# Short matmuls of constants at the head of the feed-forward up tiles of a two-layer hybrid decoder

## The chip, the cores and the metric

The kernel runs on one core of one Trainium2 chip. The metric is the device time in microseconds of one execution. Names of engines in the profile: PE is the matmul unit TensorE, PEld its weight loads, DVE is VectorE, ACT is ScalarE, POOL is GpSimd, and SP is SyncE, whose queue issues the DMAs.

## What is computed

256 tokens of width 1024 pass two layers. A layer is a half-step SwiGLU feed-forward, a mixer (stick-breaking attention in layer 0, an RG-LRU recurrent block in layer 1), and a second half-step feed-forward. Each of the six sub-layers normalises its input and modulates it by vectors made from a conditioning vector:

```python
def sublayer_input(x, g, mod_j):
    shift, scale, gate = mod_j[:, 0], mod_j[:, 1], mod_j[:, 2]
    h = rmsnorm(x, g) * (1 + scale[:, None, :]) + shift[:, None, :]
    return h, (1 + gate)[:, None, :]

def swiglu(h, w_gu, w_down):
    g, u = jnp.split(h @ w_gu, 2, axis=-1)
    return (jax.nn.silu(g) * u) @ w_down
...
        x = x + MACARON_W * g * swiglu(h, ffn_w_gu[layer, 0], ffn_w_down[layer, 0])
```

The hidden width of a feed-forward is 2816, 22 tiles of 128. Everything is float32.

## The kernel before

Activations stand with features on the 128 partitions and the 256 tokens in the columns. A product of float32 accuracy is made from three float32r matmuls: weights are split into a high part `wh` (ScalarE, L497) and a rest `wl` (VectorE, L500), activations likewise, and `group` (matmul at L526) adds wh·xh, wh·xl and wl·xh into one bank. A few products use TensorE's own float32 passes instead (`group32`, L543, and the norm's sum over partitions at L608).

A feed-forward has up tiles and a down projection. An up tile (`up`) makes one of the 22 hidden tiles: gate half and linear half side by side in one PSUM bank, eight pieces of the input each, three matmuls a piece, 2 x 8 x 3 = 48 matmuls of 256 columns, each with its own load of 128 x 128 weights. The first eight tiles of the first layer are run together, piece by piece, while their weights arrive; in the three other feed-forwards the first two tiles go through `up_first`, which starts before the norm is known, with 258 columns. That leaves 14 + 20 + 20 + 20 = 74 up tiles made by the loop in `ffn`. `swiglu_tile` then empties the bank, and `down` (also L526) sums all hidden tiles into x.

In the attention, L836 makes values, L902 scores on 64 rows of the array, L905 adds a mask by a bf16 matmul with the identity (256 columns), L929 and L931 sum over keys with constant triangles (384 and 128 columns), and L951 applies the weights. The constants that the change uses are there already: `ident` and `mask` in bf16, `ones` in float32, `ntri` and `none_` in float32r.

The order on each engine is made by a list scheduler in the kernel. Every operation is entered with an engine, a cost in ns, what it reads and what it writes; TensorE's operations get due times in program order (`nominal`, the running sum of their costs), and the others are sorted by when TensorE needs what they make. Weights arrive by DMA (L472) into 3 raw buffers; there are 7 buffers each for `wh` and `wl` of 1024 columns, and 8 banks.

Of the kernel before, what the change touches and what calls it, by code (L numbers as in the profile page):

```python
# [12 lines left out]
PSUM = bass.MemoryType.PSUM  # L13

P = 128
T = 256
TX = T + 2
D = 1024
KD = D // P
# [5 lines left out]
S = 384  # L25
# [19 lines left out]
NPAR = OFF_LAM + NR  # L45
NP0 = OFF_MB + 3 * KD  # what the first sub-layer needs

# [12 lines left out]

# [1 line left out]
class Space:  # L62
    """Memory that buffers take turns in, in program order: equal slots or an arena of cells."""

# [41 lines left out]
class Program:  # L106
# [58 lines left out]
    def schedule(self):  # L165
        ops = self.ops
        for o in ops:
            for d, data in o.deps.items():
                d.succ.append((o, data))
        # a buffer's users hold up whoever needs its place next  # L170
        spaces = {b.space for o in ops for b in o.bufs if b.space is not None}
# [33 lines left out]
        busy, gap, loads = 0.0, None, self.loads  # L205
        late = 0.0  # how far TensorE is behind its own time
        queue = {e: sorted((o for o in ops if o.eng == e), key=lambda o: (o.prio, o.seq)) for e in ("ACT", "DVE")}
# [4 lines left out]
        def guess(o, depth):  # L212
            """when an operation might start, from its inputs alone"""
            t = 0.0
            for d, data in o.deps.items():
                if d.start is not None:
                    t = max(t, d.end + self.lag(d, o, data))
                elif depth == 0:
                    return None
                else:  # L220
                    g = guess(d, depth - 1)
                    if g is None:
                        return None
                    t = max(t, max(g, free[d.eng]) + d.cost + self.lag(d, o, data))
            return t

        def wait_for(e, t, o):
            """an urgent operation, soon ready, that a start of o at t would hold up"""
            q = queue[e]
            while head[e] < len(q) and q[head[e]].start is not None:  # L230
                head[e] += 1
            n, i = 0, head[e]
            slack = o.prio + late - t
            while n < LOOK and i < len(q):
                u = q[i]
                i += 1
                if u.start is not None:
                    continue
                n += 1
                if u is o or u.prio >= o.prio:  # L240
                    break
                g = guess(u, 3)
                if g is None or g >= t + o.cost or g <= t:
                    continue
                if u.prio + late - g < o.cost and u.prio + late - g < slack - MARGIN:
                    return g
            return None
# [17 lines left out]
        while len(order) < len(ops):  # L265
# [60 lines left out]
            for b in o.bufs:  # L326
                b.uses -= 1
                if b.uses == 0 and b.space is not None:
                    sp = b.space
                    sp.live -= 1  # L330
                    # in-order engines: earlier readers on other engines have ended by their own time
                    t = o.end + 120.0 if b.hist else o.end
                    b.rel = max(getattr(b, "rel", 0.0), t)
                    for i in range(b.at, b.at + b.n):
                        sp.free[i] = b.rel
                    sp.last = max(sp.last, b.rel)
                else:
                    b.rel = max(getattr(b, "rel", 0.0), o.end + 120.0)
# [26 lines left out]
def trunk(ctx, tc, xT, cb, par, modw, gu0, gu, wdn, qk, wv, wo, win, wri, wout, out):  # L365
# [10 lines left out]

# [1 line left out]
    def ring(name, n, cols, dt=F32, pl=const):  # L378
# [52 lines left out]

# [1 line left out]
    def fixed(name, cols, dt=F32):  # L433
# [35 lines left out]

# [1 line left out]
    def dma(dst, src, n, w, after=(), lat=None):  # L471
# [10 lines left out]
    def load(src, n, name, chain=None, size=HALF):  # L482
        """n columns of weights: returns pieces of size columns, each (hi, lo)."""
        raw = Buf(rawr, name=f"raw_{name}")
# [22 lines left out]
    class Acc:  # L507
        """regions of one PSUM bank, with one start flag for the bank"""

# [4 lines left out]
        def group(self, part, o, w, wc, xs, xc, stop, parts=(None,), passes=(0, 1, 2)):  # L514
            """o += w[:, wc].T @ xs[:, xc] in three exact products"""
            b = self.b
# [21 lines left out]
    def group32(acc, part, o, w, wc, x32, xc, n, stop):  # L538
        """the same product, by TensorE's own float32 passes"""
        b = acc.b  # L540
# [8 lines left out]

# [1 line left out]
    mraw, mfin = {}, {}  # L551

    def mod_tile(l, s, w, t, after=(), lat=None):
        """row tile t of mod_w[l] for sub-layer s, part w (0 shift, 1 scale, 2 gate)."""
        key = (l, s, w)
# [12 lines left out]
    def mod_final(l, s, w, t0=0, n=KD):  # L568
# [4 lines left out]
        pp = [(pars, 0)] if l == s == 0 else [pars]  # L573
        mi = lambda: m()[:, t0 : t0 + n]  # noqa: E731
        fo = lambda: f()[:, t0 : t0 + n]  # noqa: E731
        if w == 0:
# [9 lines left out]

# [1 line left out]
    ssq, hcur, gcur = {}, {}, {}  # L588
# [27 lines left out]
    def scaled(gen, d):  # L616
        """x * scale and, in two more columns, the shift: what the first tile works on before the norm is known"""
        gs, sh = mfin[gen + (1,)], mfin[gen + (0,)]
        hi, lo = Buf(hxr), Buf(hxr)
        gcur.setdefault(gen, []).append((hi, lo))  # L620
        c = slice(d, d + 1)
        shc = lambda: sh()[:, c].to_broadcast([P, 2])  # noqa: E731
        A(lambda: hi()[:, T:], shc, AF.Copy, 2, [(sh, d)], [(hi, 1)])
# [19 lines left out]
    def down(l, s, nxt, srcs, ys, nlast, hook=None, post=None, n32=0):  # L643
        """x += gate * (W.T y) and what the next norm needs; srcs: chunks of two k tiles [P, 2, D];
        ys(k): (hi, lo), or one float32 tile for the first n32 chunks, and its columns."""
        accs = [Acc(f"acc_{l}_{s}_{i}") for i in range(5)]
# [5 lines left out]
        def step(d, k):  # L652
            acc, j = place[d]
            y, yc = ys(k)
            o = lambda b: b[:, j * T : (j + 1) * T]  # noqa: E731
            if k < 2 * n32:
# [33 lines left out]
        for ds in ((0, 1), (2, 3), (4, 5), (6,), (7,)):  # L690
# [3 lines left out]
            for d in ds:  # L694
                residual(d)

    def up(acc, ws, hx_):
        """acc = two regions of T columns: pieces of w [k, 2 P] against h"""
        for k in range(KD):
# [5 lines left out]
    def up_first(gen, ws, scale=(1.0, 1.0)):  # L705
        """the same products for the first tiles, on x * scale and shift: for each tile and region
        (tile, normed), column to add, its dependency"""
        gx = gcur.pop(gen)
# [20 lines left out]

# [1 line left out]
    def swiglu_tile(acc, y):  # L731
# [10 lines left out]
    def ffn(l, s, nxt, hook):  # L742
# [55 lines left out]
        for f in range(f0, NF):  # L798
            hook(f)
            acc = Acc(f"g_{j}_{f}")  # L800
            up(acc, load(gu[j, f], CH, f"gu_{j}_{f}", chained if j == 0 and f == f0 else None), hcur[l, s])
            swiglu_tile(acc, tile_out())
        down(l, s, nxt, [wdn[j, :, 2 * c : 2 * c + 2, :].rearrange("p k d -> p (k d)") for c in range(NF // 2)],
             lambda k: (ys[k], slice(0, T)), 2, lambda c: hook(NF + 2 * c))

# [1 line left out]
    def attention(l, s, nxt, hook):  # L807
        R, F = new_phase(88, 24)
        # softplus(-lambda) for the recurrent block, with the same tables
        A(lam, lambda: col(OFF_LAM, NR), AF.Abs, NR, [pars], [lam], after=[pr.last_pe])  # L810
# [68 lines left out]

        W2 = 2 * S  # for each of two heads: block 0 (t = 0..255), block 1 (t = 128..255)  # L880
        BL = (slice(0, T), slice(T, S))
# [7 lines left out]
        def scores(f):  # L889
            """rows are keys s, columns queries t"""  # L890
            qh, ql = qs.pop(f)
# [49 lines left out]
        def values(f):  # L941
# [13 lines left out]
            for e in range(2):  # L955
                rows = slice(e * 64, (e + 1) * 64)
                bi = lambda e=e, rows=rows: b()[rows, e * T : (e + 1) * T]  # noqa: E731
                A(lambda rows=rows: oh()[rows, :], bi, AF.Copy, T, [b], [(oh, e)], psum=True)
# [29 lines left out]

# [1 line left out]
    def rglru(l, s, nxt):  # L990
        N32 = 1  # chunks of w_out that float32 passes take
        R, F = new_phase(8 * (NB - N32), 86)
# [137 lines left out]

# [1 line left out]
    last = []  # L1132
# [73 lines left out]

# [1 line left out]
    order = pr.schedule()  # L1208
# [58 lines left out]
```

## Time and profile before

| what | value |
|---|---|
| median of the runs | 997.18 us (2 runs, 996.13 and 998.24) |
| span of the profiled execution, first to last instruction | 994.6 us |
| TensorE busy | 980.2 us (99%), 8096 matmul records |
| VectorE busy | 798.5 us (80%) |
| ScalarE busy | 561.8 us (56%) |
| HBM read | 248.92 MB |
| mean granted TensorE clock | 0.998 |

The profile describes one execution, and its page gives the span alone as that execution's time; the median lies 2.6 us above it. Busy shares are the union of overlapping records: a matmul's record is longer than the step to the next one, so the pace is read from starts, not from record lengths. The view of waits gives who waited for whom, the total, the number of times and the longest; the chain that ended last is the path from the last instruction back to the first.

### The profile page before, as it was taken

How to read it: one execution, taken by the hardware profiler on the slowest of the kernel's cores; microseconds unless marked ns; L12 is line 12 of the kernel's file. 1: busy time of each engine (PE TensorE's matmuls, PEld its weight loads, DVE VectorE, ACT ScalarE, POOL GpSimd, SP SyncE). 2: the span in 40 equal slices, each digit the busy share in tenths (PEclk: the TensorE clock that was granted, in tenths of full speed). 3: DMA queues.
4: the chain of work that ended last, by engine and by line, in shares of the span. 5: the costliest groups of instructions: out<-in, count | busy, mean ns of one | idle time of the engine just before them, and what ended most of it. 6: DMA issues, size and time to landing. Idle time of an engine off the chain costs nothing.

```text
span 994.6 us, 19696 instructions
## 1 busy us (share of the span) xinstructions
PE 980.2 (99%) x8096; PEld 969.1 (97%) x8096; DVE 798.5 (80%) x1316; ACT 561.8 (56%) x902; POOL 2.2 (0%) x14
## 2 busy tenths in 40 slices
PE   7999999999999999999999999999999999999997
PEld 5999999999999999999999999999999999999996
DVE  7997887898988999888789989874997996555433
ACT  5475443379776854444366544443779785444333
POOL 0000000000000000000000000000000000000000
PEclk9999999999999999999999999999999999999999
DMA  9988898845666389899866988886334645545421
GB/s 341 358 317 316 326 331 304 338 166 193 241 232 234 143 307 334 328 343 336 313 266 254 333 326 334 335 308 214 107 134 163 254 176 210 205 174 191 165 111 43
DMA packets 48331, 251.24 MB, mean 253 GB/s; under 512 B 5489, under 2 KB 6129, under 8 KB 28530
## 3 DMA queue, kind: packets, MB, share of 16 engines
q1 hardware_dynamic: 48242, 249.99, 68.0%
q8 instruction: 63, 1.03, 0.4%
q14 instruction: 26, 0.21, 0.1%
HBM read 248.92 MB, written 1.05 MB: 251 GB/s over the span
## 4 chain that ended last, share of the span: by engine, by line
PE 98%; DVE 1%; DMA 0%; issue 0%; ACT 0%; SPq 0%; DVEq 0%
PE bank L526 90%; PE bank L836 2%; PE bank L902 1%; PE bank L1025 1%; PE bank L951 1%; PE bank L543 1%; PE bank L929 1%; DMA x<-in_xT 0%; PE bank L905 0%; PE bank L608 0%; PE bank L931 0%; DVE x L1124 0%; DVE ssq L1151 0%; DVE rawm L564 0%; DVEq L1262 0%
## 5 line engine op out<-in xcount | busy, mean ns | idle before, releaser
L526 PE MATMUL bank<-hx,wh 128*128 128x256 f32 (+1 forms) x3392 | 606.9, 282 | 2.5 <-ACT hx L476 2.5
L497 ACT ACTIVATE wh<-raw 128x1024 fp32r<-128x1024 f32 (+1 forms) x328 | 337.2, 1046 | 339.2 <-PE bank L526 238.3
L526 PEld LDWEIGHTS bank<-hx,wh 128*128 128x128 f32 x3392 | 520.7, 189 | 4.1 <-ACT hx L476 3.3
L500 DVE TENSOR_TENSOR wl<-raw,wh 128x1024 fp32r<-128x1024 f32 (+1 forms) x328 | 390.1, 1209 | 129.4 <-ACT wh L497 126.0
L526 PE MATMUL bank<-hx,wl 128*128 128x256 f32 (+1 forms) x1696 | 475.3, 280 | 0.0
L526 PEld LDWEIGHTS bank<-hx,wl 128*128 128x128 f32 x1696 | 320.5, 189 | 0.0
L526 PE MATMUL bank<-arenar,wh 128*128 128x256 f32 x1664 | 294.7, 280 | 0.0
L526 PEld LDWEIGHTS bank<-arenar,wh 128*128 128x128 f32 x1664 | 254.1, 188 | 0.1
L526 PE MATMUL bank<-arenar,wl 128*128 128x256 f32 x832 | 232.4, 279 | 0.0
L564 DVE SCALAR_TENSOR_TENSOR rawm<-rawm,cact 128x1024 f32<-128x1024 f32 x144 | 174.8, 1219 | 19.7 <-DMA rawm<-in_modw 19.3
L526 PEld LDWEIGHTS bank<-arenar,wl 128*128 128x128 f32 x832 | 156.1, 188 | 0.0
L476 ACT ACTIVATE arenar<-a 128x256 fp32r<-128x256 f32 x88 | 35.3, 404 | 4.4 <-DVE a L735 4.4
L740 DVE TENSOR_TENSOR arenar<-a,arenar 128x256 fp32r<-128x256 f32 x88 | 36.4, 418 | 0.5 <-ACT arenar L476 0.5
L735 DVE TENSOR_TENSOR a<-bank,sg 128x256 f32<-128x256 f32 x82 | 34.1, 418 | 0.1
L476 ACT ACTIVATE sg<-bank 128x256 f32<-128x256 f32 x82 | 30.2, 368 | 6.4 <-PE bank L526 4.8
L476 ACT ACTIVATE hx<-hpre,mf 128x256 fp32r<-128x256 f32 x48 | 23.3, 501 | 16.5 <-DVE mf L577 11.1
L666 DVE SCALAR_TENSOR_TENSOR x<-bank,mf,x 128x256 f32<-128x256 f32 x48 | 21.7, 478 | 11.2 <-PE bank L526 10.8
L476 ACT ACTIVATE hx<-x,mf 128x256 fp32r<-128x256 f32 x40 | 19.0, 502 | 18.2 <-DVE x L666 18.2
L636 DVE SCALAR_TENSOR_TENSOR hx<-hpre,mf,hx 128x256 fp32r<-128x256 f32 x48 | 22.7, 479 | 2.1 <-ACT hx L476 2.1
L836 PE MATMUL bank<-wh,hx 128*128 128x256 f32 x128 | 23.7, 282 | 0.0
L476 ACT ACTIVATE arenaf<-arenaf 128x768 f32<-128x768 f32 (+1 forms) x31 | 22.0, 737 | 0.5
L634 DVE SCALAR_TENSOR_TENSOR hpre<-x,mf,rst 128x256 f32<-128x256 f32 x48 | 21.6, 479 | 0.6 <-ACT rst L476 0.4
(97 smaller groups left out, 467.7 us busy)
## 6 DMA issues: line engine op xcount, KB each, us to landing
raw<-in_gu SPq DMA_DIRECT2D x79, 1024.0 KB, 5.2
rawm<-in_modw SPq DMA_DIRECT2D x144, 512.0 KB, 6.0
raw<-in_wdn SPq DMA_DIRECT2D x44, 1024.0 KB, 4.8
raw<-in_win SPq DMA_DIRECT2D x10, 1024.0 KB, 4.8
raw<-in_qk SPq DMA_DIRECT2D x8, 1024.0 KB, 5.3
raw<-in_gu SPq DMA_DIRECT2D x14, 512.0 KB, 6.0
raw<-in_wout SPq DMA_DIRECT2D x5, 1024.0 KB, 4.9
raw<-in_wv SPq DMA_DIRECT2D x4, 1024.0 KB, 7.0
```

What stands on the lines that cost most here:

```text
L476: act.activation(o(), i(), f, **{k: (v() if callable(v) else v) for k, v in kw.items()})
L497: act.activation(h()[:, :m], raw()[:, a : a + m], AF.Copy)
L500: dve.tensor_tensor(lo()[:, :m], raw()[:, a : a + m], f32(h()[:, :m]), ALU.subtract)
L526: pe.matmul(o(b()), wc(u()), xc(v()), start=start and n == 0, stop=stop and n == len(passes) - 1, skip_group_check=True)
L543: pr.op("PE", c_mm(n, 4), lambda: pe.matmul(o(b()), wc(w()), xc(x32()), start=start, stop=stop, skip_group_check=True), [w, x32] + ([] if ...
L564: dve.scalar_tensor_tensor(raw(), raw(), 1.0, cact(), ALU.mult, ALU.mult, accum_out=m()[:, t : t + 1])
L634: V(lambda: dve.scalar_tensor_tensor(hp(), x[d](), gs()[:, c], q(), ALU.mult, ALU.mult), T, [x[d], (gs, d), q], [hp], ptr=1)
L636: V(lambda: dve.scalar_tensor_tensor(lo()[:, :T], hp(), sh()[:, c], f32(hi()[:, :T]), ALU.add, ALU.subtract), T, [hp, (sh, d), hi], [lo], ...
L666: dve.scalar_tensor_tensor(x[d](), acc.b()[:, j * T : (j + 1) * T], gate()[:, d : d + 1], x[d](), ALU.mult, ALU.add)
L735: V(lambda: dve.tensor_tensor(a(), b()[:, T:], sg(), ALU.mult), T, [(b, (1, 0)), sg], [a])
L740: V(lambda: dve.tensor_tensor(y[1](), a(), f32(y[0]()), ALU.subtract), n, [a, y[0]], [y[1]])
L836: pe.matmul(o, u()[:, tb * P : (tb + 1) * P], v()[:, c0 : c0 + 256], start=start and n == 0, stop=k == KD - 1 and n == 2, skip_group_check ...
```

## The change

A table `SHORT` has one entry for each of the 88 tiles of the four feed-forwards (22 each). Just ahead of the 48 matmuls of an up tile, the new function `short` enters a TensorE operation that writes one or several small products of constants into the tile's bank; the first of the 48 then starts the bank anew, so the products are thrown away. The kinds: "b" bf16 identity times n columns of the mask; "h" the same on 64 rows; "f" float32 ones; "r" float32r triangles; "m" several bf16 matmuls one after the other. Of the 74 tiles of the loop, 70 get an entry that is not empty: 14 in the first feed-forward, 19, 19 and 18 in the others. The comments of the file are stripped too, which moves line numbers only: L526 of before is L534 of after, for instance.

```diff
+SHORT = [(None, 0)] * 8
+SHORT += [("b", n) for n in range(1, 15)]
+SHORT += [(None, 0)] * 3 + [("b", n) for n in (15, 16, 17, 31, 33, 47, 49, 63, 65, 95, 97, 127, 129, 255)] + [("h", n) for n in (1, 2, 3, 4, 65)]
+SHORT += [(None, 0)] * 3 + [("f", n) for n in range(1, 11)] + [("r", n) for n in (2, 4, 6, 8, 10, 12, 34, 66, 98)]
+SHORT += [(None, 0)] * 3 + [("m", n) for n in ((1, 1), (1, 1, 1), (1, 2), (3, 3, 3), (5, 5, 5, 5), (7,) * 8, (65, 65), (33,) * 3, (129,) * 2,
+                                               (128, 1), (1, 128), (64, 63), (255, 255))] + [("b", 1), ("b", 3), ("f", 1), (None, 0), ("b", 2), ("b", 1)]
...
+    def short(acc, i):
+        kind, n = SHORT[i]
+        if kind is None:
+            return
+        def fn():
+            o = acc.b()
+            if kind == "b":
+                pe.matmul(o[:, :n], ident, mask[:, :n], start=True, stop=True)
+            elif kind == "h":
+                pe.matmul(o[:, :n], ident[:64, :], mask[:64, :n], start=True, stop=True)
+            elif kind == "f":
+                pe.matmul(o[:, :n], ones, ones[:, :n], start=True, stop=True)
+            elif kind == "r":
+                pe.matmul(o[:, :n], ntri, none_[:, :n], start=True, stop=True)
+            else:
+                for m in n:
+                    pe.matmul(o[:, :m], ident, mask[:, :m], start=True, stop=True)
+        pr.op("PE", 120.0, fn, [], [acc.b])
...
         for f in range(f0, NF):
             hook(f)
             acc = Acc(f"g_{j}_{f}")
+            short(acc, j * NF + f)
             up(acc, load(gu[j, f], CH, f"gu_{j}_{f}", chained if j == 0 and f == f0 else None), hcur[l, s])
             swiglu_tile(acc, tile_out())
```

TensorE at the head of the first up tile of the loop in the first feed-forward (tile 8, entry "b" with one column), before:

```order
L526 MATMUL bank_65<-hx_105,wh_82 128x256
L526 MATMUL bank_65<-hx_106,wh_82 128x256
L526 MATMUL bank_65<-hx_105,wl_89 128x256
L526 MATMUL bank_66<-hx_91,wh_83 128x256
L526 MATMUL bank_66<-hx_92,wh_83 128x256
```

And now:

```order
L534 MATMUL bank_65<-hx_105,wh_82 128x256
L534 MATMUL bank_65<-hx_106,wh_82 128x256
L534 MATMUL bank_65<-hx_105,wl_89 128x256
L714 LDWEIGHTS ident
L714 MATMUL bank_66<-mask,ident 128x1
L534 MATMUL bank_66<-hx_91,wh_83 128x256
L534 MATMUL bank_66<-hx_92,wh_83 128x256
```

A weight load and a matmul stand between the last matmul of one tile (bank 65) and the first of the next (bank 66); nothing else moves here. The other heads stand in the same way at their tiles.

The 120 ns that the scheduler counts for each entry shift what it does elsewhere. VectorE in the first feed-forward, where the products of the modulation rows (`rawm`, `mr`), the weight splits (`wl`) and the rests of finished hidden tiles (`arenar`) take turns, before:

```order
L735 TENSOR_TENSOR a_131<-bank_69,sg_128 128x256
L564 SCALAR_TENSOR_TENSOR rawm_76,mr_169<-rawm_76,cact 128x1024
L500 TENSOR_TENSOR wl_84<-raw_71,wh_77 128x1024
L740 TENSOR_TENSOR arenar_755<-a_131,arenar_755 128x256
L564 SCALAR_TENSOR_TENSOR rawm_74,mr_169<-rawm_74,cact 128x1024
L500 TENSOR_TENSOR wl_85<-raw_72,wh_78 128x1024
```

And now:

```order
L764 TENSOR_TENSOR a_131<-bank_69,sg_128 128x256
L572 SCALAR_TENSOR_TENSOR rawm_76,mr_169<-rawm_76,cact 128x1024
L572 SCALAR_TENSOR_TENSOR rawm_74,mr_169<-rawm_74,cact 128x1024
L508 TENSOR_TENSOR wl_84<-raw_71,wh_77 128x1024
L769 TENSOR_TENSOR arenar_755<-a_131,arenar_755 128x256
L508 TENSOR_TENSOR wl_85<-raw_72,wh_78 128x1024
```

A modulation row comes one place earlier and a split one place later. There are some dozens of such exchanges on VectorE, ScalarE and the load queue, all within a few places. On TensorE one place changes its order, two heads of scores in the attention; before:

```order
L902 MATMUL bank_67<-arenar_2427 128x256 x3
L902 MATMUL bank_67<-arenar_2427 128x128 x3
L905 LDWEIGHTS ident
L905 MATMUL bank_67<-mask,ident 128x2x128
L836 MATMUL bank_66<-wh_82,hx_97 128x256
L836 MATMUL bank_66<-wl_89,hx_97 128x256
L836 MATMUL bank_66<-wh_82,hx_98 128x256
L836 MATMUL bank_66<-wh_82,hx_97 128x256
L836 MATMUL bank_66<-wl_89,hx_97 128x256
L836 MATMUL bank_66<-wh_82,hx_98 128x256
L902 MATMUL bank_68<-arenar_2427 128x256 x3
```

And now:

```order
L866 MATMUL bank_66<-wh_82,hx_97 128x256
L866 MATMUL bank_66<-wl_89,hx_97 128x256
L866 MATMUL bank_66<-wh_82,hx_98 128x256
L932 MATMUL bank_67<-arenar_2447 128x256 x3
L932 MATMUL bank_67<-arenar_2447 128x128 x3
L935 LDWEIGHTS ident
L935 MATMUL bank_67<-mask,ident 128x2x128
L932 MATMUL bank_68<-arenar_2447 128x256 x3
```

The six value matmuls that stood between the two heads now stand ahead of both.

## The prediction

> **What bounds the kernel now.** I read the busy shares first, then the chain that ended last, then the waits of TensorE, and last the pace of its matmuls in the trace.
>
> ```profile
> span 994.6 us, 19696 instructions
> PE 980.2 (99%) x8096; PEld 969.1 (97%) x8096; DVE 798.5 (80%) x1316; ACT 561.8 (56%) x902; POOL 2.2 (0%) x14
> PEclk9999999999999999999999999999999999999999
> ...
> PE 98%; DVE 1%; DMA 0%; issue 0%; ACT 0%; SPq 0%; DVEq 0%
> ```
>
> A busy share of 99% alone would say little, since matmul records overlap. The chain says more: 98% of the span is led by one matmul releasing the next. The granted clock is full in every slice. TensorE's own waits are these, all of them:
>
> ```profile
> PE bank L1168 <- DMA rawm<-in_cb: 4.1, 1, 4.1
> PE bank L526 <- ACT hx L476: 2.5, 1, 2.5
> PE bank L608 <- DVE ssq L1151: 0.6, 1, 0.6
> PE bank L608 <- ACT sq L476: 0.2, 1, 0.2
> ```
>
> That is 7.4 us, nearly all of it before the first feed-forward tile. After that TensorE never stops for data. So whatever is put into its queue lengthens the kernel by what it takes there, unless it changes how fast the rest flows. The pace is read from the chain in order of time (start, length, engine, number of matmuls):
>
> ```profile
> 334.35 186.94 PE bank L526 x1584
> 521.73 186.93 PE bank L526 x1584
> ...
> 804.67 181.19 PE bank L526 x1536
> ```
>
> 186.94 us / 1584 = **0.118 us per matmul** of 256 columns, and 181.19 / 1536 = 0.118 in the last layer. These three stretches are the three feed-forward layers after the first one, up tiles and down projections together; each up tile is 48 such matmuls, 5.66 us. A profile is one execution: span 994.6 us, against a median of 997.18 us for the runs shown, so 2.6 us lie around the span. I add the sum below to 997.18.
>
> **The change, part by part.** Nothing is removed. Of 74 up tiles outside the first-tile scheme, 70 get a short matmul or a run of them; 94 matmuls in all. By kind: 32 bf16 matmuls alone in their tile ("b"), 5 bf16 on 64 rows ("h"), 11 float32 ("f"), 9 float32r ("r"), and 13 tiles with runs of 2 to 8 bf16 matmuls, 37 together ("m"). None waits for anything but the bank that the tile's first matmul waits for today. The table of waits shows no wait of L526 on a bank's readers, so the earlier claim on the bank costs nothing.
>
> *One bf16 matmul (b).* The nearest row is the one bf16 matmul the kernel has, L905 in the attention, 256 columns between float32r ones. Start, length, engine, line:
>
> ```profile
> 219.07 0.28 PE L836 MATMUL bank<-wh,hx 128*128 128x256 f32 x1
> 219.27 0.90 PE L902 MATMUL bank<-arenar 64*128 64x256 f32 x6
> 220.11 0.28 PE L905 MATMUL bank<-mask,ident 128*128 128x256 bf16 x1
> 220.15 0.37 PE L836 MATMUL bank<-wh,hx 128*128 128x256 f32 x1
> 220.35 0.28 PE L836 MATMUL bank<-wl,hx 128*128 128x256 f32 x1
> ```
>
> From L905's start to the start of the second L836 behind it are 0.24 us; one L836 takes 0.118 at its pace, which leaves 0.12 for L905. The start stamped at 220.15 is no real start: that row lasts 0.37 where the next lasts 0.28, so it stood for 0.09 behind L905. Fewer columns should cost less, but not in proportion, because each matmul brings a weight load, and the load of the tile's first big matmul stands behind it. Small matmuls with a load each are seen in the scans of the attention:
>
> ```profile
> 227.67 0.51 PE L929 MATMUL bank<-arenar,ntri 128*128 128x384 f32 x2
> 228.01 0.33 PE L931 MATMUL bank<-arenar,none 128*128 128x128 f32 x2
> 228.19 0.57 PE L929 MATMUL bank<-arenar,ntri 128*128 128x384 f32 x2
> 228.59 0.33 PE L931 MATMUL bank<-arenar,none 128*128 128x128 f32 x2
> ```
>
> Two matmuls of 128 columns hold the queue from 228.01 to 228.19, 0.09 each by the stamps, and the first L929 of the second pair lasts 0.06 longer than those of the first pair (0.57 against 0.51), so up to 0.12 each in truth. That is no less than a matmul of twice the columns: the weights set it. I take **0.11 us** for a lone bf16 matmul whatever its columns; the bounds are 0.06 (128 columns at half the 256-column pace) and 0.127 (L905 with all of its stretch).
>
> What enters from float32r into bf16 is not shown alone: L902 to L905 changes the rows of the array too. Its bound is that change of rows, worked out under h, up to 0.19. I take nothing for it, because the way back out of bf16 (L905 to L836) shows next to nothing.
>
> The Trainium skill ("TensorE: Matmul & The Clock Gate", section "Back-to-back issue gap") has about 25 ns as the smallest start-to-start time of small matmuls. By it 94 short matmuls would be an estimated 2.4 us. The two L931 of this trace speak against it, at 0.09 each; but their weights are float32, which the same page (section "Weight-path perf modes — Fast Weight Load (FWL) and DoubleRow") leaves out of its fast loads.
>
> *64 rows (h).* L836 takes 0.20 from 219.07 to L902 instead of 0.118: 0.08 more. The six L902 take 0.84 to L905, where three of 256 and three of 128 columns would take 3 x 0.118 + 3 x (0.06 to 0.118) = 0.53 to 0.71: 0.13 to 0.31 more. In and out together 0.21 to 0.39, so one change of rows is 0.10 to 0.19. I take 0.29 plus the 0.11: 0.40 each, bounds 0.27 and 0.52.
>
> *float32 (f).* One instruction leaves two records. The row of the chain is
>
> ```profile
> 768.97 6.91 PE bank L543 x32
> ```
>
> 6.91 / 32 = 0.216 per record at 256 columns. With 1 to 10 columns I price both records at the small-matmul price: 0.23, bounds 0.12 and 0.43.
>
> *float32r (r).* As L931: 0.11, bounds 0.06 and 0.12. *Runs (m).* The last of each run pays the 0.11 before the big weights; the 24 others share one stationary operand with the next and load bf16. The load records of the attention show what a bf16 load is beside a float32 one:
>
> ```profile
> 220.10 0.10 PEld L905 LDWEIGHTS <-ident 128*128 128x128 bf16 x1
> 220.11 0.20 PEld L836 LDWEIGHTS bank<-wh,hx 128*128 128x128 f32 x1
> ```
>
> 0.10 against 0.20 us: half. So 0.06 each for these 24, bounds 0 and 0.12.
>
> The **sum**: 32 x 0.11 = 3.5; 5 x 0.40 = 2.0; 11 x 0.23 = 2.5; 9 x 0.11 = 1.0; 13 x 0.11 + 24 x 0.06 = 2.9. Together **11.9 us**. All low bounds: 54 x 0.06 + 5 x 0.27 + 11 x 0.12 = 5.9 us. All high bounds: 54 x 0.125 + 5 x 0.52 + 11 x 0.43 + 24 x 0.12 = 17.0 us, and with 0.19 more at 45 entries into bf16, 25.5 us.
>
> *What is moved.* The planner gives each short matmul 120 ns, and so orders conversions, splits and loads a little differently: a modulation row's product a place earlier, a split a place later, one pair of scores in the attention behind more value matmuls (same number of row changes). I cost this at nothing. What covers it is how far the producers run ahead:
>
> ```profile
> ACT wh L497 <- PE bank L526: 238.3, 125, 3.7
> ```
>
> ```profile
> L500 DVE TENSOR_TENSOR wl<-raw,wh x328: 683/1224/1229, 12.4 to 969.5; 128x1024 fp32r<-128x1024 f32 x160, 128x512 fp32r<-128x512 f32 x4
> ```
>
> The first row is a wait (who, for whom, us in total, times, longest), the second the weight splits (shortest, median, longest ns). ScalarE stood 238 us, in 125 places, because TensorE had not yet freed a weight buffer: weights are converted long before they are used. A split that comes one place later comes 1.2 us later. Without that cover, it would cost up to 1.2 us a place. ScalarE and VectorE meet a tile that ends 0.1 us later, which gives them more room, not less.
>
> **The rivals.**
>
> *The stream changes its pace (faster).* A float32 matmul is four passes in the code's own terms (c_mm with 4), and two records of 0.216 make 0.108 per pass of 256 columns. A float32r pass takes 0.118. If these 0.010 us hang on a phase between array and operand reads which a short matmul, above all one of odd columns, sets anew, then 70 tiles x 48 x 0.010 = 33.6 us would go, less 11.9: 975.5 us. To be 20 us (2%) ahead net of the cost, a tile must save (20 + 11.9) / 70 = 0.46 us, nearly the full 0.48; if the state lasted into the down projections, less would do. For it: every moving operand so far has an even number of columns, so the trace has never tried the other state. Against it: the pace is 0.118 in all three stretches, which come behind the attention's bf16 matmuls, behind float32 ones and behind 128 and 384 columns; two L929 of 384 columns take 0.34 us, 0.44 ns a column against 0.46, so the excess grows with the columns and looks like the price of reading float32r. Chance 0.06.
> The page named above has 256 / 2.4 + 2.5 = 109 ns for such a matmul, an estimate near the float32 pass; the 118 of this trace do not agree with it.
>
> *Entering bf16 is dear (slower).* If the array must empty before it turns from float32r to bf16, as it seems to for 64 rows, the 45 entries cost 0.19 each, 8.6 us more; with the other terms at their high bounds the time is 997.2 + 25.5 = 1022.7 us, 2.6% slower. It decides from 20 us / 70 = 0.28 us per tile. For it: the change from L902 to L905 is one of type as well as of rows. Against: L905 to L836 shows no such thing. A phase that makes the pace worse would end on this side as well. Chance 0.12.
>
> *The short ones vanish in the queue.* If all weight loads run far enough ahead, a short matmul costs its columns only. All heads together have about 3,000 columns; at the stream's 0.118 / 256 = 0.46 ns a column that is 1.4 us, 998.6 us; halfway to the forecast's low bound it would be 1001. For it: the load of a bf16 block is the shorter one. Against it are the two L931. Chance 0.08.
>
> *The new order starves a place.* A split late at three or four transitions between layers: 4 x 1.2 = 5 us more, 1014 us. Chance 0.09.
>
> **How the numbers follow.** The forecast, with 0.65 (the faster pace has 0.06, the dear entry 0.12, the vanishing case 0.08, the starved place 0.09), is 997.2 + 11.9 = **1009 us**, 1.2% slower; its own range by the bounds is 1003 to 1014. From 998 to 1021 lie the forecast, the starved place, the vanishing case and a third of the dear entry; outside are the faster pace with 0.06, the other two thirds of the dear entry with 0.08, and 0.03 for what I have not thought of: 0.17. Two per cent, about what a measurement of this kernel can tell from no change, is 977.2 to 1017.1. Faster 0.06; slower 0.12, the dear entry; the rest, 0.82, is within.
>
> **What would show it.** In the profile after: 8,096 + 94 + 11 = 8,201 matmul records of TensorE (a float32 matmul leaves two); its waits still under 8 us in sum; a tile of 48 still 5.66 us from first to last big matmul, with odd and even, bf16 and float32 heads alike; between the last matmul of one tile and the first real start of the next 0.2 to 0.25 us instead of 0.118, and 0.5 for h. Wrong would be: tiles whose pace depends on the head's columns; a head of 0.3 us or more for plain bf16; new waits of TensorE on weights or banks inside a layer.

## The result, and the profile after

The changed kernel takes 1010.31 us (median of 2 runs, 1009.15 and 1011.46) against 997.18 us: a ratio of **1.0134**, 95% interval 1.0095 to 1.0172. The interval leaves no room for "no change": the kernel is slower, by 13.1 us, but by less than the 2% from which a change counts as slower here. The forecast was 1009 us.

The page of the changed kernel: span, busy time, and the chain that ended last by engine.

```profile
span 1009.5 us, 19903 instructions
PE 993.7 (98%) x8201; PEld 978.5 (97%) x8201; DVE 797.9 (79%) x1316; ACT 562.5 (56%) x902; POOL 2.2 (0%) x14
PEclk9999999999999999999999999999999999999999
...
PE 96%; DMA 1%; DVE 1%; ACT 1%; issue 0%; SPq 0%; DVEq 0%
```

The 8201 matmul records are the 8096 of before, the 94 of the heads and one more for each of the 11 float32 ones. The clock is full throughout. The chain is still TensorE's, but a little of it (2%) now runs over DMA, VectorE and ScalarE; that is taken up below. The chain in order of time (start, length) in the first feed-forward and in the last one:

```profile
91.80 5.77 PE bank L534 x48
97.59 5.76 PE bank L534 x48
103.38 5.77 PE bank L534 x48
109.17 5.78 PE bank L534 x48
...
926.94 5.77 PE bank L534 x48
932.73 67.97 PE bank L534 x576
```

The chain of before had one piece in place of these, 1536 matmuls in the last feed-forward, and this one over the whole of the first:

```profile
13.05 195.14 PE bank L526 x1632
```

Now each tile stands alone between its heads: 5.79 us from tile to tile, against 48 x 0.118 = 5.66. The head at 97.4 has 7 columns, the one at 103.2 has 8, and both tiles behind them take the same time. Behind the last head, 576 matmuls take 67.97 us, 0.118 each as before.

One head of each kind as the timeline of TensorE shows it (start, length, line, operands, number):

```profile
97.30 0.28 PE L534 MATMUL bank<-hx,wl 128*128 128x256 f32 x1
97.41 0.18 PE L714 MATMUL bank<-mask,ident 128*128 128x7 bf16 x1
97.45 0.48 PE L534 MATMUL bank<-hx,wh 128*128 128x256 f32 x2
97.77 0.28 PE L534 MATMUL bank<-hx,wl 128*128 128x256 f32 x1
...
430.35 0.28 PE L534 MATMUL bank<-hx,wl 128*128 128x256 f32 x1
430.56 0.17 PE L716 MATMUL bank<-mask,ident 64*128 64x1 bf16 x1
430.66 0.51 PE L534 MATMUL bank<-hx,wh 128*128 128x256 f32 x2
431.01 0.28 PE L534 MATMUL bank<-hx,wl 128*128 128x256 f32 x1
...
569.50 0.28 PE L534 MATMUL bank<-hx,wl 128*128 128x256 f32 x1
569.62 0.28 PE L718 MATMUL bank<-ones 128*128 128x6 f32 x2
569.76 0.49 PE L534 MATMUL bank<-hx,wh 128*128 128x256 f32 x2
570.09 0.27 PE L534 MATMUL bank<-hx,wl 128*128 128x256 f32 x1
```

From one `wl` row to the next are three steps of the stream, 0.354 us, where no head stands between. Here they are 0.47 (bf16), 0.66 (64 rows) and 0.59 (float32): the heads cost 0.12, 0.31 and 0.24. The first big matmul is stamped only 0.04 us after the bf16 head (97.45 against 97.41), but that stamp is again no real start: the `wh` pair that begins there lasts 0.48 where a pair lasts 0.40 elsewhere. Read in this way (over six steps, to even out their scatter), all 70 heads come to:

| kind | forecast, each | measured, each | forecast, us | measured, us |
|---|---|---|---|---|
| 32 lone bf16, 1 to 255 columns | 0.11 | 0.125 (0.117 to 0.134) | 3.5 | 4.00 |
| 5 on 64 rows | 0.40 | 0.31 | 2.0 | 1.54 |
| 11 float32 | 0.23 | 0.23 | 2.5 | 2.53 |
| 9 float32r | 0.11 | 0.11 | 1.0 | 1.00 |
| 13 runs, 37 bf16 | 0.11 + 0.06 for each inner one | 0.15 for two of one column, 0.305 for eight of 7, 0.23 for two of 255 | 2.9 | 2.42 |
| all 70 | | | 11.9 | 11.5 |

The span grew by 14.9, so 3.4 us are not the heads'.

### The profile page after: what moved, and what is told of

Its sections match the earlier page's. It is cut to its first block, busy times and chain, and to the rows that moved or that the text cites. A ratio compares the mean times of both kernels' runs of the same rounds, so it can differ in the third digit from the quotient of the medians.

```text
span 1009.5 us, 19903 instructions
## 1 busy us (share of the span) xinstructions
PE 993.7 (98%) x8201; PEld 978.5 (97%) x8201; DVE 797.9 (79%) x1316; ACT 562.5 (56%) x902; POOL 2.2 (0%) x14
## 4 chain that ended last, share of the span: by engine, by line
PE 96%; DMA 1%; DVE 1%; ACT 1%; issue 0%; SPq 0%; DVEq 0%
PE bank L534 88%; PE bank L866 2%; PE bank L932 1%; PE bank L1055 1%; PE bank L981 1%; DMA rawm<-in_modw 1%; PE bank L551 1%; DMA raw<-in_win 1%; PE bank L959 1%; PE bank L935 0%; PE bank L961 0%; DVE hx L644 0%; PE bank L616 0%; DVE x L1154 0%; ACT wh L505 0%
## 5 line engine op out<-in xcount | busy, mean ns | idle before, releaser
L534 PE MATMUL bank<-hx,wh 128*128 128x256 f32 (+1 forms) x3392 | 617.4, 284 | 3.7 <-ACT hx L484 3.1
L534 PEld LDWEIGHTS bank<-hx,wh 128*128 128x128 f32 x3392 | 521.6, 189 | 6.4 <-ACT hx L484 3.8
L534 PE MATMUL bank<-hx,wl 128*128 128x256 f32 (+1 forms) x1696 | 475.4, 280 | 0.0
L534 PEld LDWEIGHTS bank<-hx,wl 128*128 128x128 f32 x1696 | 320.5, 189 | 0.0
L534 PE MATMUL bank<-arenar,wh 128*128 128x256 f32 x1664 | 294.7, 279 | 0.0
L534 PEld LDWEIGHTS bank<-arenar,wh 128*128 128x128 f32 x1664 | 254.2, 188 | 0.1
L534 PE MATMUL bank<-arenar,wl 128*128 128x256 f32 x832 | 232.6, 280 | 0.0
L534 PEld LDWEIGHTS bank<-arenar,wl 128*128 128x128 f32 x832 | 156.1, 188 | 0.0
```

Of the source, the lines that this page charges most:

```text
L534: pe.matmul(o(b()), wc(u()), xc(v()), start=start and n == 0, stop=stop and n == len(passes) - 1, skip_group_check=True)
```

## The experiments

The theory at this point: the heads cost TensorE 11.5 us, and what a head costs is the load of the float32 weights behind it. The rivals: the new order costs something; the same weights are not loaded twice; a change between big and small matmuls has a fixed price; the stream itself is bound by its weight loads.

**The heads in the old order.** The heads are counted at 0 ns, by which every other instruction keeps its place of before.

```diff
-        pr.op("PE", 120.0, fn, [], [acc.b])
+        pr.op("PE", 0.0, fn, [], [acc.b])
```

> The heads as in the changed kernel, but the scheduler counts them with 0 ns, so that every engine keeps the order of the kernel before and only the 168 weight loads and matmuls of the heads are new. Theory A (the heads cost TensorE time, 11.5 us by the trace of the changed kernel; the rest of its 14.9 us of span is one late piece in the recurrent block, 1.2 us, that came with the new order, and 2.0 us ahead of the first head that have nothing to do with the change): heads 11.5 us again, no lateness near the recurrent block, median 11 to 13 us above the kernel before. Rival B (the new order costs the rest): heads 11.5 us, and everything beside them within 0.3 us of the kernel before, the start included.

1008.76 us (4 runs) against 997.53 (13 runs of the kernel before on the same chip), 1.011, interval 1.0094 to 1.0127: 11.2 us slower. The heads again come to 11.5 us, and the start was 0.0 us late. The recurrent block was 0.5 us late, which theory A had not expected in this order.

**The new order without heads.**

```diff
-        pr.op("PE", 120.0, fn, [], [acc.b])
+        pr.op("PE", 120.0, lambda: None, [], [acc.b])
```

> The order of the changed kernel on every engine, with the heads counted at 120 ns but not issued. Theory A: the 1.2 us in the recurrent block come back, nothing else does; median 0 to 3 us above the kernel before. Rival B: the 2.0 us at the start come back as well, 3 us above. Rival C (the order costs nothing; it was the heads that pushed a piece late): within 0.3 us of the kernel before inside the layers.

998.39 us (10 runs) against 997.53 (13): 1.0004, 0.9995 to 1.0014. The new order without heads costs nothing that these runs can tell from zero; the interval leaves room for up to 1.4 us. Inside the layers no piece is late: theory A's 1.2 us in the recurrent block did not come back, as rival C had forecast. The start was 1.8 us late, which was rival B's forecast.

**Runs with the weights the same or in turn.** Order of before, in every loop tile a head, one kind for each feed-forward:

```diff
+            if j == 0:
+                pe.matmul(o[:, :2], w[0][0]()[:, :P], none_[:, :2], start=True, stop=True)
+            elif j == 1:
+                for m in range(8):
+                    pe.matmul(o[:, :2], ntri, none_[:, :2], start=True, stop=True)
+            elif j == 2:
+                for m in range(8):
+                    pe.matmul(o[:, :2], (ntri, none_)[m % 2], none_[:, :2], start=True, stop=True)
             else:
+                for m in range(8):
+                    pe.matmul(o[:, :2], (ident, mask[:, :P])[m % 2], mask[:, :2], start=True, stop=True)
```

> Order of before; every up tile of the loop has a head, one kind for each feed-forward. First: one float32r matmul of 2 columns that uses the very weights block that the tile's first big matmul uses next. Second: 8 float32r matmuls of 2 columns with one and the same triangle as weights. Third: the same 8 with two triangles in turn. Fourth: 8 bf16 matmuls of 2 columns with two bf16 blocks in turn. Theory W (a short matmul costs the load of the weights that come behind it, float32 0.11 us, bf16 0.025, loaded anew each time): 0.11; 8 x 0.11 = 0.9; 0.9; 7 x 0.025 + 0.12 = 0.3 us a tile. Rival S (a load is saved when the weights are the same as before, and that is why the inner matmuls of the bf16 runs took 0.025): 0.03; 7 x 0.03 + 0.11 = 0.3; 0.9; 0.9 us. Rival F (a fixed price of a switch between big and small matmuls, whatever the weights): 0.11; 0.3; 0.3; 0.3 us.

The timeline of TensorE in the first, second and fourth feed-forward of this kernel:

```profile
72.71 0.28 PE L527 MATMUL bank<-hx,wl 128*128 128x256 f32 x1
72.83 0.17 PE L704 MATMUL bank<-none,wh 128*128 128x2 f32 x1
72.85 0.49 PE L527 MATMUL bank<-hx,wh 128*128 128x256 f32 x2
73.18 0.28 PE L527 MATMUL bank<-hx,wl 128*128 128x256 f32 x1
...
355.33 0.28 PE L527 MATMUL bank<-hx,wl 128*128 128x256 f32 x1
355.45 0.95 PE L707 MATMUL bank<-none,ntri 128*128 128x2 f32 x8
356.26 0.48 PE L527 MATMUL bank<-hx,wh 128*128 128x256 f32 x2
356.58 0.28 PE L527 MATMUL bank<-hx,wl 128*128 128x256 f32 x1
...
860.35 0.28 PE L527 MATMUL bank<-hx,wl 128*128 128x256 f32 x1
860.48 0.18 PE L713 MATMUL bank<-mask,ident 128*128 128x2 bf16 x1
860.51 0.16 PE L713 MATMUL bank<-mask 128*128 128x2 bf16 x1
860.54 0.16 PE L713 MATMUL bank<-mask,ident 128*128 128x2 bf16 x1
...
860.69 0.48 PE L527 MATMUL bank<-hx,wh 128*128 128x256 f32 x2
861.01 0.28 PE L527 MATMUL bank<-hx,wl 128*128 128x256 f32 x1
```

The head with the tile's own weights costs 73.18 - 72.71 - 0.354 = 0.12. Eight float32r matmuls with one triangle cost 1.25 - 0.354 = 0.90; over the 20 tiles of each kind they come to 0.89 on average, with one triangle and with two in turn alike. Eight bf16 ones with two blocks in turn start some 0.025 apart and cost 861.01 - 860.35 - 0.354 = 0.306, on average 0.303. All heads together come to 14 x 0.115 + 40 x 0.89 + 20 x 0.303 = 43.3 us; the one run took 1041.26 us, 43.7 more than the kernel before. Theory W gave 0.11, 0.9, 0.9 and 0.3, and holds; rival S fell with the first two numbers, rival F with the second. In this program each matmul has a weight-load instruction of its own, and it is paid even when the weights are the same. A float32r block takes 0.112 us (the step inside the float32r runs) where a bf16 one takes at most 0.025. That it is the load and not the short matmul is seen in the bf16 runs: the same matmul costs 0.025 with a bf16 block behind it and 0.125 with a float32r block behind it. A price of leaving bf16 is not needed for this, since a float32r head costs 0.11 as well. By the Trainium skill ("TensorE: Matmul & The Clock Gate", section "LDWEIGHTS (loading the stationary operand)") 128 columns of weights take an estimated 107 ns; the 112 of this run lie 5% above it. The Trainium skill's 25 ns as the smallest step between small matmuls (section "Back-to-back issue gap" of that page) agrees with the bf16 runs, and only with these.

**Fewer columns of input, fewer of weights.** Kernel before, no heads; pieces 1 to 7 of an up tile take `nn` of 256 columns (second feed-forward) or `mm` of 128 columns of weights (third), so the kernel leaves out parts of the products:

```diff
-                group(acc, (g, 0), lambda b, g=g: b[:, g * T : (g + 1) * T], ws[k // 4],
-                      lambda u, c0=c0: u[:, c0 : c0 + P], hx_[k], lambda v: v[:, :T], T, k == KD - 1)
+                nn, mm = (n, m) if k else (T, P)
+                group(acc, (g, 0), lambda b, g=g, nn=nn, mm=mm: b[:mm, g * T : g * T + nn], ws[k // 4],
+                      lambda u, c0=c0, mm=mm: u[:, c0 : c0 + mm], hx_[k], lambda v, nn=nn: v[:, :nn], T, k == KD - 1)
```

> Kernel before without heads; in the second feed-forward the up tiles take only n columns of the input for pieces 1 to 7 (n from 16 to 254, another n in each tile), in the third the weights of those pieces have only 64, 32 or 96 of 128 columns; so parts of the products are left out. Theory W: the pace falls with n only to the float32 weight load, near 0.11 us, and stays there down to 16 columns; 0.118 at 256 is set by the columns, so it stays 0.118 with 64 columns of weights. Rival L (the stream at 256 columns is bound by the weight load as well): 0.118 at every n, and shorter with fewer columns of weights. Rival M (matmuls cost their columns only): n x 0.46 ns, 0.03 us at 64.

Timeline rows of the tiles with 16, 208 and 252 columns:

```profile
349.05 0.26 PE L526 MATMUL bank<-hx,wl 128*128 128x16 f32 x1
349.16 0.37 PE L526 MATMUL bank<-hx,wh 128*128 128x16 f32 x2
349.38 0.26 PE L526 MATMUL bank<-hx,wl 128*128 128x16 f32 x1
...
449.77 0.27 PE L526 MATMUL bank<-hx,wl 128*128 128x208 f32 x1
449.88 0.39 PE L526 MATMUL bank<-hx,wh 128*128 128x208 f32 x2
450.11 0.28 PE L526 MATMUL bank<-hx,wl 128*128 128x208 f32 x1
...
481.33 0.28 PE L526 MATMUL bank<-hx,wl 128*128 128x252 f32 x1
481.44 0.40 PE L526 MATMUL bank<-hx,wh 128*128 128x252 f32 x2
481.68 0.28 PE L526 MATMUL bank<-hx,wl 128*128 128x252 f32 x1
```

Three steps take 0.33 and 0.34 us with 16 and with 208 columns, 0.35 with 252. The mean steps of whole tiles are 0.112 us from 200 to 240 columns, 0.1145 at 248, 0.117 at 252 and 0.118 at 254. With 96, 64 and 32 columns of weights and all 256 of input they are 0.118, 0.1175 and 0.1165. So 0.112 us, the load of the runs above, is the floor, and it is the columns that hold the stream 0.006 above it: theory W again, against rivals L and M. Between 32 and 176 columns the step was 0.213, because the clock was at half there (last section); that is also why the one run took 1034.41 us, longer than the kernel before.

**The same two kernels again**, for the 3.4 us that the heads don't explain.

> The kernel before, once more, for the spread of single pieces between two executions of one program. The runs so far: the stretch up to the 96th matmul of TensorE is 1.8 us later in the changed kernel and in its order without heads, and 0.0 to 0.5 us later in three kernels with the order of before, although no order differs there; the place in the recurrent block is 1.2 us later in the changed kernel, 0.5 with the heads in the old order, 0 in the new order without heads. Theory N (the start is chance of the DMAs): the start differs from the first profile of the same kernel by up to 2 us in either kernel; the recurrent block by nothing here. Rival O (the start belongs to the program): within 0.3 us of its first profile.

> The changed kernel, once more. Theory N: heads 11.5 us again to a tenth; start anywhere from 0 to 2 us later than the first profile of the kernel before; the recurrent block late by 0.5 to 1.5 us if the heads cause it, by anything from 0 if it is chance too. Rival O: start 1.8 us and recurrent block 1.2 us late once more.

> The kernel before a third time. Theory N: its start up to 2 us from that of its first profile, its recurrent block unchanged. Rival O: both within 0.3 us.

> The changed kernel a third time. Theory N: heads 11.5 us, start 0 to 2 us late, recurrent block 0 to 1.5 us late. Rival O: 1.8 and 1.2 us late as in its first profile.

The heads took 11.5 us in each profile of the changed kernel. The first 384 matmuls, counted from TensorE's first one, against the first profile of before (all ahead of the first head):

| kernel | later by, first 384 matmuls | later by, recurrent block |
|---|---|---|
| before, second and third profile | 1.4, 0.2 | 0.0, 0.0 |
| changed, three profiles | 1.8, 0.7, 2.0 | 1.2, 0.0, 0.1 |
| heads in the old order | 0.0 | 0.5 |
| new order without heads | 1.8 | 0.0 |
| runs of short matmuls, fewer columns (both in the old order) | 0.5, 0.7 | 0.0, 0.0 |

Theory N's forecast came, and rival O fell: the start moves by up to 1.4 us between profiles of one and the same kernel. The profile of before that the forecast started from had one of the earliest starts. That the start is chance alone is not shown, though. The four profiles in the new order start 0.7 to 2.0 us late, the five further ones in the old order 0.0 to 1.4. Up to 60 us, where the 384 matmuls end, neither an engine nor the load queue has its instructions in another order than before, so the order gives no cause for it; why the new one starts later on average stays open. The two late places of the first profile, 1.8 and 1.2, make 3.0 of the 3.4 us. The chain of the changed kernel names what came late at the start, and, from 714.17 on, in the recurrent block:

```profile
2.97 7.13 DMA rawm<-in_modw
...
14.18 19.59 PE bank L534 x145
...
714.17 1.15 DVE wl L508
715.34 6.81 DMA raw<-in_win
722.17 1.06 ACT wh L505
723.23 0.40 ACT hx L484
```

In the first profile of before TensorE's stream begins at 13.05. In the recurrent block a load of 1 MB took 6.81 us. The page of before has such loads (number, size, median us from issue to landing) at 4.8:

```profile
raw<-in_win SPq DMA_DIRECT2D x10, 1024.0 KB, 4.8
```

ScalarE could convert that block only when it had landed (722.17) and went on to the normed input `hx` only after that (723.23), and TensorE waited for `hx` in pieces, 1.2 us in all. The lateness follows this one load from profile to profile: 6.81 us and 1.2 late, 6.10 and 0.5 (heads in the old order), 5.66 and 0.1 (third profile of the changed kernel), and 4.64 to 4.85 with nothing late in the seven others. So a slow load made the place late. The three slow ones are among the five profiles with heads and none is among the five without; whether heads make it likelier stays open.

## Why the prediction was right, point by point

- *TensorE bounds, and what stands in its queue adds to the end.* Right: 11.5 us of heads, 11.2 us between the medians of the cleanest comparison.
- *A lone bf16 matmul costs 0.11 whatever its columns.* Right in kind, 0.125 in size, close to the 0.12 that the row of L905 gave and to the upper bound of 0.127. I had gone between it and the half-size L931; the nearest row alone would have been better.
- *No price for entering bf16.* Nearly right: float32r heads cost 0.111, bf16 ones 0.125, so a change of type, in and out together, is worth some 0.014, not 0.19. The dear entry fell.
- *64 rows.* Above a lone bf16 head these cost 0.31 - 0.125 = 0.185, a little under the range of 0.21 to 0.39 for both changes of rows; I took its middle, 0.5 us too much for the five. No run takes the 0.185 apart.
- *Inner matmuls of the runs.* 0.025 with few columns, 0.057 with 129 and 0.108 with 255, 0.033 on average, not 0.06. What went wrong was to price them by half a load record's length; a record's length is not the step between loads. It came to 0.5 us too much for the runs.
- *The stream keeps its pace.* Right: odd, even, bf16, float32, 64 rows, and 0.118 behind each. The faster pace would have needed 5.2 us tiles; they stayed at 5.66 plus the head.
- *The new order costs nothing.* Right as far as it can be told: 1.0004, with room for up to 1.4 us. A late place in the recurrent block was seen in one profile of the changed kernel of three (0.1 us in another), but it was a slow load, not a split that stands a place later.
- *Its waits under 8 us.* Missed: they came to 8.5, 7.5 and 8.5 us in the three profiles. But the second profile of the kernel before has 8.2, so 8 us was too close a bound to show anything of the change. In the first profile 0.5 of it are waits for `hx` behind the slow load.
- *The sum.* It is 0.4 us from the heads, closer than its terms: 0.5 too little for the lone ones, 0.5 too much for 64 rows and 0.5 too much for the runs. That two of them cancel is luck. That the medians differ by 13.1 rather than 11.5 fits the late starts in the new order (0.7 to 2.0 us in the profiles) and the slow load, but no run shows it. The chances add up to 1.03 with the 0.03 for what was not thought of.

## What to carry to other kernels

On an engine that never waits, price an added instruction by the step from a row ahead of it to a row behind it, not by its record: here the record of the next matmul took the cost, and its stamped start hid it. A short matmul in front of float32r weights cost that weight load, 0.11 to 0.13 us, for 1 to 255 columns alike; in front of a bf16 block one of few columns cost 0.025. Before a difference of 1 or 2 us in a single profile gets a cause, profile the same program again.

## What the runs showed of the hardware that was not expected

The clock fell to half while TensorE was issuing without a gap, in the kernel with fewer columns. Its stretches (start:end, PE busy with records, granted clock, DMA share, GB/s):

```profile
342.00:347.00 5.00, 5.00 (x46) 1.00 0.60 210
349.00:353.00 4.00, 4.00 (x25) 0.65 0.81 297
365.00:374.00 9.00, 9.00 (x44) 0.50 0.26 96
416.00:425.00 9.00, 9.00 (x44) 0.50 0.48 181
444.00:447.50 3.50, 3.50 (x33) 1.00 0.95 396
```

TensorE is busy for all of each stretch by its records. With 16 columns every 0.112 us the granted clock went from 1.00 to 0.50 and stayed there through tiles of 32 to 176 columns, each step 0.213 us; it came back in the tile of 192. So a full row of records did not keep the clock up here. The columns that stream in the time seem to count: the tile of 176 columns every 0.213 us ended at half clock, and in the next one, of 192, the clock came back. Both changes of the clock were seen once, in one profile, and no run tests another order of the tiles. The page of the Trainium skill named above (Part 1, "The HAM clock gate (the "warmup" mystery)") ties the gate to how busy the array was in recent windows of about 3.4 us; the rows agree if busy means columns streamed. At half clock the load's floor about doubled, from 0.112 to 0.213 us. The heads, 0.1 to 0.3 us in every 5.9, never brought the clock down, nor did the eight float32r matmuls of 0.89 us a tile (granted clock 0.998 in both kernels).

Also unexpected: loading the same float32r weights again one behind the other saves nothing (0.112 each), and a float32r matmul streams 0.46 ns a column (0.118 us for 256), where a float32 pass, half of a 0.216 us record, takes 0.108 us for 256 and the inner bf16 matmul of 255 columns 0.108, 0.42 ns each.
